# A conditioning product's last sum moved from the matrix engine to GpSimd, and its bias carried by another transposition

## The chip, the cores and the metric

The kernel runs on one core of a Trainium2 chip. The metric is the time of one execution on the device in microseconds (us); for a set of runs the median is given. Engines are named as the profile names them: PE (TensorE's matrix products), PEld (its weight loads, which overlap the products), DVE (VectorE), ACT (ScalarE), POOL (GpSimd), and SP (SyncE), which only issues transfers here. An entry such as SPq is the instruction queue of that engine. L482 is line 482 of the kernel.

## What is computed

One layer of a diffusion trunk with 1024 latent tokens, 256 context tokens and width 1024, all in float32. The part that matters here is the modulation: one vector of 6144 numbers, made from the conditioning vector `c`, that shifts, scales and gates the rest of the layer.

```python
mod = jax.nn.silu(c) @ ada_w[l] + ada_b[l]          # (1, 1024) @ (1024, 6144)
sh1, sc1, g1, sh2, sc2, g2 = jnp.split(mod, 6, axis=-1)
hx = modulate(rms_norm(x, norm1_g[l]), sh1, sc1)     # h * (1 + scale) + shift
out_x, _ = mixer_block(hx, lp, ctx_states, True)     # projection, conv group, RWKV group, projection
x = x + g1 * out_x
hx = modulate(rms_norm(x, norm2_g[l]), sh2, sc2)
x = x + g2 * conv_ffn(hx, lp, rows, GRID_W)
return rms_norm(x, final_g)
```

`sh1` and `sc1` are needed at once (and for the context tokens too). The other four, `g1, sh2, sc2, g2`, are needed later: `g1` at the output projection, `sh2` and `sc2` at the second normalization, `g2` at the very end.

## The kernel before, in words

The kernel works in stages: a start in which the inputs are normalized and `sh1, sc1` are made; the projections (`proj`, L354), in which each weight column block of 128 is multiplied in three passes of high and low halves; the decays and the inversion of small triangular matrices for the RWKV group (`decays`, `invert`); sixteen steps of the scan; the output projection; and the gated MLP (L1104, L1184).

Instructions are written in program order, and a planner in the framework lays them out at build time: it simulates the engines with its own costs and fixes the order in which each engine, and each engine's queue of transfers, will take its instructions. On the chip every engine keeps that order and waits at each instruction for what it needs. So an instruction that is planned too early holds up everything behind it on its engine, and a changed instruction can change the planned order elsewhere.

**The rest of the modulation** (`ada_rest`, L456 to L491) makes `g1, sh2, sc2, g2` in eight groups of 512 columns, numbered 4 to 11. It is a generator: the list `OR1` calls one group at a time between the column blocks of the first projections. For each group the 1024 rows of the weight come in as four transfers (`araw`, L466) of two row sets each. Row set k of the weight is multiplied by the k-th set of the conditioning vector and added to one of two accumulators of 128 x 512: accumulator 0 by DVE (L471, four additions; ACT makes the first product at L469), accumulator 1 by ACT and POOL (ACT scales, L473; POOL adds, L474, two additions). What is left is a sum over the 128 partitions, and over the two accumulators, which PE does with a vector of ones:

- in a **column group** (6 to 9: `sh2` and `sc2`) each 128 columns of each accumulator are loaded as weights and multiplied by the column of ones, and a third product adds the bias from a one-row tile `row`; the three accumulate in PSUM (L482, L483), and DVE copies the four columns out (L484). Every such float32 product shows as two records in the trace.
- in a **row group** (4, 5, 10, 11: `g1` and `g2`) the ones are the weights and the accumulators the moving data, 512 columns each (L487); DVE adds the bias row (L488), and the row goes to DRAM (L489).

The bias row is fetched by SP for all eight groups (L461) into `arow`, of which there are two.

**The small parameters** are fetched at the start by twelve transfers on POOL's queue (L278 to L290) into three blocks `pr` of 128 rows, which PE transposes (L292 to L294) and DVE copies into the tile `prm` (L295 to L299). Rows 78 to 93 of the first block are the bias of groups 0 to 3. `prm` is needed for the first modulation: L244, L255, then `gs1` (L316), then the modulated input (ACT L326), which the projections read.

`sp` (L104 to L106) splits a weight in two halves: ACT makes the high one, POOL the low one (`wlo`), which the projections use.

Of the kernel before, what the change touches and what calls it, by code (L numbers as in the profile page):

```python
# [8 lines left out]
F32 = mybir.dt.float32  # L9
F32R = mybir.dt.float32r  # L10
AF = mybir.ActivationFunctionType
ALU = mybir.AluOpType
# [25 lines left out]
PADC, PADM = 88, 80  # L38
# [49 lines left out]
def hybrid_kernel(  # L88
# [7 lines left out]
    V, A, G, PE, SY = nc.vector, nc.scalar, nc.gpsimd, nc.tensor, nc.sync  # L96

    PQ = G
# [9 lines left out]
    cp = ctx_.enter_context(tc.tile_pool(name="cp", bufs=1, side="left"))  # L108
# [18 lines left out]
    ident = cst[:, C_ID:C_ID + 128]  # L127


    prm = cp.tile([128, 292], F32, name="prm")  # L130
    P_N1, P_N2, P_KK, P_KA, P_RK, P_CW, P_FB, P_FW, P_LB, P_AB = 0, 8, 16, 20, 24, 28, 40, 62, 260, 276
    kac = cp.tile([128, 4], F32, name="kac")

    modc = cp.tile([128, 4, 8, 2], F32, name="modc")
# [2 lines left out]
    ccs = cp.tile([128, 8, 2], F32, name="ccs")  # L137
    eps6, epsg = 1e-6, 64e-5

    cp.tile([128, PADC], F32, name="padc")  # L140


    kd_ = dr.tile([4, 128, TT], F32, name="k_dram")
# [62 lines left out]
    with ExitStack() as s2:  # L206
# [15 lines left out]
        acc = [np_.tile([128, 512], F32, name=f"aacc{t}") for t in range(2)]  # L222
# [53 lines left out]
        pr = np_.tile([128, 3, 128], F32, name="pr")  # L276
        V.memset(pr, 0.0)
        PQ.dma_start(pr[0:8, 0, :], norm1_g[0].rearrange("(j p) -> j p", p=128))  # L278
        PQ.dma_start(pr[78:94, 0, :], ada_b[0, 0:2048].rearrange("(j p) -> j p", p=128))
        PQ.dma_start(pr[8:16, 0, :], norm2_g[0].rearrange("(j p) -> j p", p=128))  # L280
        PQ.dma_start(pr[16:20, 0, :], rw_k_k[0].rearrange("(j p) -> j p", p=128))
        PQ.dma_start(pr[20:24, 0, :], rw_k_a[0].rearrange("(j p) -> j p", p=128))
# [8 lines left out]
        pt = pp.tile([128, 512], F32, name="ptr", tag="pcol", bufs=1)  # L291
# [1 line left out]
        PE.transpose(pt[:, 128:256], pr[:, 1, :], ident)  # L293
        PE.transpose(pt[:, 256:384], pr[:, 2, :], ident)  # L294
        V.tensor_copy(prm[:, 0:62], pt[:, 0:62])  # L295
        V.tensor_copy(prm[:, P_AB:P_AB + 16], pt[:, 78:94])
        V.tensor_copy(prm[:, 62:161], pt[:, 128:227])
        V.tensor_copy(prm[:, 161:260], pt[:, 256:355])
        V.tensor_scalar(out=prm[:, P_LB:P_LB + 16], in0=pt[:, 62:78], scalar1=0.5, scalar2=None, op0=ALU.mult)  # L299
# [3 lines left out]
        for o in XO:  # L303
# [4 lines left out]
            else:  # L308
                ci = int(o)
                load_ada(ci, i_[ci])  # L310
                i_[ci] += 1
        while n_ < NT:
# [4 lines left out]
                               in1=prm[:, P_N1:P_N1 + 8].unsqueeze(2).to_broadcast([128, 8, 2]), op0=ALU.add, op1=ALU.mult)  # L317
        for g, (t0, n, w) in enumerate(segs3):
            for q in range(2):
                o = [seg_tile(g, q, i, F32R) for i in range(2)]  # L320
                hxt[g, q, 0], hxt[g, q, 1] = o
                for jj in range(4):
                    j = 4 * q + jj
# [43 lines left out]
    ad = sa.enter_context(tc.tile_pool(name="ad", bufs=1, side="right", reuse_waits="tile"))  # L367
# [88 lines left out]
    def ada_rest():  # L456
        kinds = {4: ("row", 0), 5: ("row", 0), 6: ("col", 2), 7: ("col", 2), 8: ("col", 3), 9: ("col", 3), 10: ("row", 1), 11: ("row", 1)}
        for ci in range(4, 12):
            src = ada_w[0, :, ci * 512:(ci + 1) * 512].rearrange("(p k) n -> p k n", k=8)
            row = ad.tile([1, 512], F32, name="arow", bufs=2)  # L460
            SY.dma_start(row, ada_b[0:1, ci * 512:(ci + 1) * 512])  # L461
            acc = [ad.tile([128, 512], F32, name=f"acc{e}", bufs=2) for e in range(2)]
            for k in range(8):
                if k % 2 == 0:
                    raw = ad.tile([128, 2, 512], F32, name="araw", bufs=AR)
                    SY.dma_start(raw, src[:, k:k + 2, :])  # L466
                e, z = AE[k], acc[AE[k]]
                if k == AE.index(e):
                    A.activation(z, raw[:, k % 2, :], AF.Identity, scale=ccs[:, k, 0:1])  # L469
                elif e == 0:  # L470
                    V.scalar_tensor_tensor(out=z, in0=raw[:, k % 2, :], scalar=ccs[:, k, 0:1], in1=z, op0=ALU.mult, op1=ALU.add)  # L471
                else:
                    A.activation(raw[:, k % 2, :], raw[:, k % 2, :], AF.Identity, scale=ccs[:, k, 0:1])  # L473
                    G.tensor_tensor(out=z, in0=z, in1=raw[:, k % 2, :], op=ALU.add)  # L474

            ps = pa_.tile([128, 512], F32, name="pada", tag="pa", bufs=2)
            one = cst[:, C_ONE:C_ONE + 1]
            half, (what, i) = ci % 2, kinds[ci]
            if what == "col":
                for b in range(4):  # L480
                    for e in range(2):
                        PE.matmul(ps[:, b:b + 1], acc[e][:, 128 * b:128 * b + 128], one, start=(e == 0), stop=False)  # L482
                    PE.matmul(ps[:, b:b + 1], row[:, 128 * b:128 * b + 128], one[0:1, :], start=False, stop=True)  # L483
                V.tensor_copy(modc[:, i, 4 * half:4 * half + 4, 0], ps[:, 0:4])  # L484
            else:
                for e in range(2):
                    PE.matmul(ps[0:1, :], one, acc[e], start=(e == 0), stop=(e == 1))  # L487
                V.tensor_tensor(out=row, in0=ps[0:1, :], in1=row, op=ALU.add)  # L488
                SY.dma_start(gd[i][:, 512 * half:512 * half + 512], row)  # L489
            yield  # L490
        V.scalar_tensor_tensor(out=gs2, in0=modc[:, 3, :, 0], scalar=1.0, in1=prm[:, P_N2:P_N2 + 8], op0=ALU.add, op1=ALU.mult)  # L491

    pa_ = Banks(pa=PA)
    ada_ = ada_rest()
    un = unit_k()
    for o in OR1.split():
# [558 lines left out]
    for r in range(16):  # L1055
# [3 lines left out]
        if r == RC:  # L1059
            fill(999)  # L1060
            sa.close()
            op = so.enter_context(tc.tile_pool(name="op", bufs=1, side="left", reuse_waits="tile"))
# [67 lines left out]
    for f in (1, 0, *range(2, NF)):  # L1130
# [12 lines left out]
        acc = up.tile([128, 16, 64], F32, name="acc", bufs=2)  # L1143
        for tap in range(9):
            a_, b_ = divmod(tap, 3)
# [9 lines left out]
        for hf, c0, n, t0 in PIECES:  # L1155
            V.tensor_tensor(out=act[:, t0:t0 + n], in0=pv[hf][:, c0:c0 + n],  # L1156
                            in1=acc.rearrange("p r c -> p (r c)")[:, t0:t0 + n], op=ALU.mult)
# [93 lines left out]
```

## Time and profile before

| | |
|---|---|
| median of 3 runs | 1708.09 us (1707.33 to 1716.09) |
| the profiled execution's own time | 1706.38 us |
| its span, first to last instruction | 1704.6 us |
| mean granted clock of TensorE | 0.94 of full |
| busiest engines over the span | PE 91%, DVE 67%, ACT 36%, POOL 33% |

The profile is of one execution of its own. Its time is 1.8 us more than the span, and the span is what the rows below divide. The busy shares are averages over stages with different limits, so the rows below are read by stage.

### The profile page before, as it was taken

What the parts mean: (1) busy time and instruction counts of PE and PEld (TensorE: products, weight loads), DVE (VectorE), ACT (ScalarE), POOL (GpSimd) and SP (SyncE); (2) the same over time, 40 slices, a digit from 0 to 9 for tenths busy, and PEclk for the clock granted to TensorE, in tenths of its full rate; (3) what the DMA queues carried; (4) which work ended last, traced back from release to release, by engine and by line L of the source; (5) the groups of instructions that cost most, each with busy time, mean ns of one, the idle gap of its engine ahead of it and who ended that gap; (6) DMA issues with size and microseconds to landing.
All of it is one profiled execution on the core that took longest, in us unless ns stands there. A gap on an engine that the chain in (4) does not pass through costs nothing.

```text
span 1704.6 us, 27504 instructions
## 1 busy us (share of the span) xinstructions
PE 1557.3 (91%) x10639; PEld 1258.8 (74%) x10639; DVE 1148.5 (67%) x1783; ACT 619.2 (36%) x1158; POOL 562.6 (33%) x489
## 2 busy tenths in 40 slices
PE   7699999989899866899778889999999999999997
PEld 2588768867777656787666668888888888788886
DVE  4954525798899987444677577777777777446645
ACT  2654315544445335444345331211111111324323
POOL 2343312332333303412444322222222222545643
PEclk9699799989799976999889999999999999999999
DMA  9385536557576487988652211111111111533521
GB/s 320 105 292 170 182 95 208 164 152 247 159 231 209 135 248 221 331 249 279 188 164 85 92 50 50 50 50 48 43 46 50 50 50 50 178 106 124 173 93 57
DMA packets 233147, 246.94 MB, mean 145 GB/s; under 512 B 18483, under 2 KB 171656, under 8 KB 233016
## 3 DMA queue, kind: packets, MB, share of 16 engines
q1 hardware_dynamic: 232632, 245.02, 46.1%
q8 instruction: 84, 1.38, 0.3%
q14 instruction: 47, 0.39, 0.1%
q0 software_dynamic: 384, 0.15, 0.0%
HBM read 178.79 MB, written 66.33 MB: 144 GB/s over the span
## 4 chain that ended last, share of the span: by engine, by line
PE 68%; DVE 17%; DMA 7%; ACT 3%; issue 3%; POOL 2%; SPq 1%; DVEq 0%; ACTq 0%; POOLq 0%
PE pf L1104 26%; PE pj L354 13%; PE pf L1184 12%; PE pco L906 2%; DVE ti L672 2%; DVE tmp L670 2%; PE po L906 2%; PE px L601 2%; DMA araw<-in_ada_w_dram 2%; DVE acc L1151 2%; PE ry L760 1%; PE pu L772 1%; PE ps L784 1%; DMA vu<-v_dram 1%; PE ry L752 1%
## 5 line engine op out<-in xcount | busy, mean ns | idle before, releaser
L1104 PE MATMUL pf<-h,fhi 128*128 128x512 f32 x1408 | 385.1, 390 | 6.7 <-DVE act L1156 4.1
L1104 PEld LDWEIGHTS pf<-h,fhi 128*128 128x128 f32 x1408 | 265.0, 188 | 63.1 <-DVE act L1156 4.5
L354 PE MATMUL pj<-hx,whi 128*128 128x512 f32 (+1 forms) x976 | 301.6, 388 | 0.9 <-DVE hx L328 0.9
L1151 DVE SCALAR_TENSOR_TENSOR acc<-gp,prm,acc 128x1024 f32<-128x1024 f32 x176 | 272.7, 1551 | 6.0
L106 POOL TENSOR_TENSOR flo<-fraw,fhi 128x1024 fp32r<-128x1024 f32 x50 | 124.2, 2485 | 306.0 <-ACT fhi L105 305.9
L1104 PE MATMUL pf<-h,flo 128*128 128x512 f32 x704 | 223.7, 390 | 0.0
L354 PEld LDWEIGHTS pj<-hx,whi 128*128 128x128 f32 x976 | 184.0, 196 | 37.2 <-issue 4.2
L354 PE MATMUL pj<-hx,wlo 128*128 128x512 f32 (+1 forms) x488 | 189.0, 388 | 0.0
L1184 PE MATMUL pf<-dhi,ahl 128*128 128x512 f32 x640 | 163.0, 389 | 0.2 <-DVE ahl L1176 0.2
L1176 DVE TENSOR_TENSOR ahl<-act,ahl 128x512 fp32r<-128x512 f32 x44 | 86.2, 1969 | 100.2 <-ACT ahl L1175 100.2
L1104 PEld LDWEIGHTS pf<-h,flo 128*128 128x128 f32 x704 | 132.5, 188 | 27.5 <-POOL flo L106 0.2
L105 ACT CAST fhi<-fraw 128x1024 fp32r<-128x1024 f32 x50 | 52.7, 1054 | 266.7 <-issue 158.6
L1184 PEld LDWEIGHTS pf<-dhi,ahl 128*128 128x128 f32 x640 | 120.0, 188 | 25.5 <-DVE ahl L1176 0.6
L106 POOL TENSOR_TENSOR dlo<-fraw,dhi 128x1024 fp32r<-128x1024 f32 x40 | 98.6, 2469 | 92.2 <-ACT dhi L105 88.2
L106 POOL TENSOR_TENSOR wlo<-wraw,whi 128x1024 fp32r<-128x1024 f32 x26 | 63.6, 2447 | 159.9 <-ACT whi L105 159.8
L354 PEld LDWEIGHTS pj<-hx,wlo 128*128 128x128 f32 x488 | 95.7, 196 | 17.2 <-issue 1.7
L1149 DVE TENSOR_SCALAR acc<-gp,prm 128x1024 f32<-128x1024 f32 x22 | 42.5, 1932 | 97.3 <-ACT gp L1141 97.3
L650 POOL TENSOR_TENSOR car<-car,pcs 128x512 f32<-128x512 f32 (+1 forms) x38 | 39.3, 1046 | 152.4 <-DMA car<-ar_dram 102.1
L1184 PE MATMUL pf<-dlo,ahl 128*128 128x512 f32 x320 | 89.1, 389 | 0.0
L601 PE MATMUL px<-arO,kbO 64*128 64x128 f32 (+1 forms) x640 | 63.9, 310 | 18.1 <-DVE xrO L605 12.7
L105 ACT CAST dhi<-fraw 128x1024 fp32r<-128x1024 f32 x40 | 41.9, 1050 | 105.0 <-PE pf L1184 87.4
L601 PEld LDWEIGHTS px<-arO,kbO 64*128 64x128 f32 x640 | 51.9, 207 | 34.6 <-issue 28.9
(292 smaller groups left out, 2651.2 us busy)
## 6 DMA issues: line engine op xcount, KB each, us to landing
araw<-in_ada_w_dram SPq DMA_DIRECT2D x48, 512.0 KB, 5.5
fraw<-in_ffn_w_up_dram SPq DMA_DIRECT2D x46, 512.0 KB, 3.8
fraw<-in_ffn_w_down_dram SPq DMA_DIRECT2D x44, 512.0 KB, 3.7
wraw<-in_w_in_dram SPq DMA_DIRECT2D x26, 512.0 KB, 4.5
lu<-lu_dram SPq DMA_DIRECT2D x20, 512.0 KB, 5.2
kb_dram<-kbT SPq DMA_DIRECT2D x40, 256.0 KB, 2.6
xa_dram<-xa SPq DMA_DIRECT2D x20, 512.0 KB, 5.6
cxa<-xa_dram SPq DMA_DIRECT2D x40, 256.0 KB, 3.8
```

Of the source, the lines that this page charges most:

```text
L105: A.copy(hi, src)
L106: G.tensor_tensor(out=lo, in0=src, in1=hi.bitcast(F32), op=ALU.subtract)
L354: PE.matmul(p[:, :n], w[:, k, :], hsl(i, k, t0, n), start=(k == 0 and first), stop=(k == 7 and last))
L601: PE.matmul(px[:, ch, i, 0:w], kbO[r, i, 2 * ch:2 * ch + 2, :].rearrange("p s n -> p (s n)"), rhs, start=True, stop=True)
L650: F3.tensor_tensor(out=self.ar, in0=self.ar, in1=self.pc.to_broadcast(list(self.ar.shape)), op=ALU.mult)
L670: V.tensor_tensor(out=tv, in0=ti[:, j + 1:32, j:j + 1].to_broadcast([128, m, j]), in1=ti[:, j:j + 1, 0:j].to_broadcast([128, m, j]), op=AL ...
L906: m = PE.matmul(po, hl[:, a_, k, :], w[k][b_][:, sl], start=(k == 0 and f), stop=(k == 3 and l))
L1104: PE.matmul(pts[hf], w[:, k, :], h2[hf][i_][:, k, :], start=(k == 0 and f), stop=(k == 7 and l))
L1149: V.tensor_scalar(out=acc, in0=src, scalar1=wcol, scalar2=prm[:, P_FB + f:P_FB + f + 1], op0=ALU.mult, op1=ALU.add)
L1151: V.scalar_tensor_tensor(out=acc, in0=src, scalar=wcol, in1=acc, op0=ALU.mult, op1=ALU.add)
L1176: V.tensor_tensor(out=hl[:, 1, :], in0=asl, in1=hl[:, 0, :].bitcast(F32), op=ALU.subtract)
L1184: PE.matmul(pd[i], hl[:, a_, 128 * q:128 * q + 128], w[w_][:, 512 * nh:512 * nh + 512], start=(f == 0 and s_), stop=(f == NF - 1 and l_))
```

## The change

POOL gets a third addition per group, which adds accumulator 1 to accumulator 0 when both are done. PE then sums one accumulator where it summed two. The column groups' bias, 2048 numbers, no longer comes as rows through SP and a third product: one more transfer on POOL's queue puts it in rows 94 to 109 of the first parameter block, it passes through the same transposition, the copy to `prm` is 32 columns wide where it was 16, and DVE adds it when it takes the four columns from PSUM. The row groups keep their bias row. `prm` grows by 16 columns and a padding tile shrinks by as many.

```diff
-    prm = cp.tile([128, 292], F32, name="prm")
+    prm = cp.tile([128, 308], F32, name="prm")
...
-    cp.tile([128, PADC], F32, name="padc")
+    cp.tile([128, PADC - 16], F32, name="padc")
...
         PQ.dma_start(pr[78:94, 0, :], ada_b[0, 0:2048].rearrange("(j p) -> j p", p=128))
+        PQ.dma_start(pr[94:110, 0, :], ada_b[0, 3072:5120].rearrange("(j p) -> j p", p=128))
...
-        V.tensor_copy(prm[:, P_AB:P_AB + 16], pt[:, 78:94])
+        V.tensor_copy(prm[:, P_AB:P_AB + 32], pt[:, 78:110])
...
         for ci in range(4, 12):
             src = ada_w[0, :, ci * 512:(ci + 1) * 512].rearrange("(p k) n -> p k n", k=8)
-            row = ad.tile([1, 512], F32, name="arow", bufs=2)
-            SY.dma_start(row, ada_b[0:1, ci * 512:(ci + 1) * 512])
+            half, (what, i) = ci % 2, kinds[ci]
+            if what == "row":
+                row = ad.tile([1, 512], F32, name="arow", bufs=2)
+                SY.dma_start(row, ada_b[0:1, ci * 512:(ci + 1) * 512])
...
+            G.tensor_tensor(out=acc[0], in0=acc[0], in1=acc[1], op=ALU.add)
...
             one = cst[:, C_ONE:C_ONE + 1]
-            half, (what, i) = ci % 2, kinds[ci]
             if what == "col":
                 for b in range(4):
-                    for e in range(2):
-                        PE.matmul(ps[:, b:b + 1], acc[e][:, 128 * b:128 * b + 128], one, start=(e == 0), stop=False)
-                    PE.matmul(ps[:, b:b + 1], row[:, 128 * b:128 * b + 128], one[0:1, :], start=False, stop=True)
-                V.tensor_copy(modc[:, i, 4 * half:4 * half + 4, 0], ps[:, 0:4])
+                    PE.matmul(ps[:, b:b + 1], acc[0][:, 128 * b:128 * b + 128], one, start=True, stop=True)
+                a_ = P_AB + 16 + 4 * (ci - 6)
+                V.tensor_tensor(out=modc[:, i, 4 * half:4 * half + 4, 0], in0=ps[:, 0:4], in1=prm[:, a_:a_ + 4], op=ALU.add)
             else:
-                for e in range(2):
-                    PE.matmul(ps[0:1, :], one, acc[e], start=(e == 0), stop=(e == 1))
+                PE.matmul(ps[0:1, :], one, acc[0], start=True, stop=True)
                 V.tensor_tensor(out=row, in0=ps[0:1, :], in1=row, op=ALU.add)
```

## Rows read from the trace of the kernel before

**Rows 1.** The page's engines: busy us, share of the span, instructions.

```profile
PE 1557.3 (91%) x10639; PEld 1258.8 (74%) x10639; DVE 1148.5 (67%) x1783; ACT 619.2 (36%) x1158; POOL 562.6 (33%) x489
```

**Rows 2.** Busy time by stretch (columns named in the first line).

```profile
core 0: us, PE busy (x) PEld busy (x) DVE busy (x) ACT busy (x) POOL busy (x), PEclk, DMA share, GB/s
0.00:76.00 76.00, 49.23 (x196) 27.12 (x197) 51.02 (x130) 32.32 (x61) 25.96 (x31) 0.82 0.73 232
...
76.00:250.00 174.00, 174.00 (x837) 135.14 (x836) 84.54 (x130) 69.41 (x118) 49.76 (x32) 0.93 0.55 176
...
250.00:314.00 64.00, 62.78 (x374) 51.12 (x373) 31.23 (x65) 31.36 (x61) 18.81 (x31) 1.00 0.68 208
314.00:600.00 286.00, 258.39 (x2188) 211.04 (x2188) 267.84 (x627) 135.38 (x256) 103.75 (x153) 0.92 0.60 184
```

**Rows 3.** Chain of waits, 76 to 314 us: shares of these 238 us by line.

```profile
by line: PE pj L354 73.4%; PE px L601 3.8%; PE pb L439 3.6%; PE pada L482 3.5%; PE pada L487 3.2%; PE psm L421 3.1%; PE pv L452 2.5%; PE pada L483 2.2%; PE pt L609 1.7%; PE plo L556 0.8%; PE plo L555 0.8%; PE prn L432 0.5%; PE pst L426 0.4%
```

**Rows 4.** Tile `pada`: instructions, duration in ns (min/median/max), starts, forms.

```profile
L482 PE MATMUL pada<-cst,acc x64: 164/250/352, 146.6 to 203.1; 128*128 128x1 f32 x64
...
L483 PE MATMUL pada<-cst,arow x32: 245/266/365, 147.0 to 203.6; 1*128 1x1 f32 x32
...
L487 PE MATMUL pada<-acc,cst x16: 590/592/954, 109.5 to 231.2; 128*1 128x512 f32 x16
...
L484 DVE COPY modc<-pada x4: 150/164/164, 149.9 to 204.2; 128x4 f32<-128x4 f32 x4
...
L244 DVE TENSOR_TENSOR modc<-pada,prm x1: 157/157/157, 40.0 to 40.0; 128x8 f32<-128x8 f32 x1
```

**Rows 5.** Timeline of PE: start us, us, what; in brackets the idle time before.

```profile
33.03 1.95 PE L243 MATMUL pada<-cst,aacc 128*128 128x1 f32 x16
34.84 0.31 PE L292 MATMUL ptr<-cst,pr 128*128 128x128 f32 x1
...
38.95 0.33 PE L294 MATMUL ptr<-cst,pr 128*128 128x128 f32 x1
...
44.79 3.68 PE L273 MATMUL ph<-cst,xt 128*128 128x128 f32 x16
...
109.49 1.88 PE L487 MATMUL pada<-acc,cst 128*1 128x512 f32 x4
...
229.42 1.02 PE L487 MATMUL pada<-acc,cst 128*1 128x512 f32 x2
```

**Rows 6.** Timeline of POOL.

```profile
7.77 0.57 POOL L290 DMA_DIRECT2D pr<-in_ffn_conv_w_dram  x1 [0.31 <-DMA pr<-in_rw_k_k_dram]
...
99.79 1.29 POOL L474 TENSOR_TENSOR acc<-acc,araw 128x512 f32<-128x512 f32 x1 [2.90 <-ACT araw L473]
...
118.10 2.41 POOL L106 TENSOR_TENSOR wlo<-wraw,whi 128x1024 fp32r<-128x1024 f32 x1 [3.24 <-ACT whi L105]
...
131.87 2.39 POOL L106 TENSOR_TENSOR wlo<-wraw,whi 128x1024 fp32r<-128x1024 f32 x1 [5.84 <-ACT whi L105]
```

**Rows 7.** Timeline of DVE and of ACT.

```profile
45.51 0.17 DVE L316 SCALAR_TENSOR_TENSOR gs<-modc,prm 128x16 f32<-128x16 f32 x1
...
118.68 2.38 DVE L471 SCALAR_TENSOR_TENSOR acc<-araw,ccs,acc 128x512 f32<-128x512 f32 x1 [4.97 <-ACT acc L469]
...
212.74 0.73 DVE L471 SCALAR_TENSOR_TENSOR acc<-araw,ccs,acc 128x512 f32<-128x512 f32 x1
...
46.28 2.07 ACT L326 ACTIVATE hx<-hx,modc,gs 128x256 fp32r<-128x256 f32 x4
```

**Rows 8.** SP's queue, 0 to 260 us: who waited for whom, us, times, longest.

```profile
SPq L461 <- PE pada L483: 6.1, 4, 2.5
```

**Rows 9.** Busy time by stretch, 160 to 220 us (columns as in group 2).

```profile
160.00:220.00 60.00, 60.00 (x271) 45.23 (x272) 28.72 (x52) 21.80 (x37) 16.88 (x11) 0.80 0.48 150
```

**Rows 10.** Transfers issued from 0 to 60 us: count, KB each, median us to landing.

```profile
pr<-in_ffn_conv_w_dram POOLq DMA_DIRECT2D x2, 49.5 KB, 5.4
```

## The prediction

> **What bounds the kernel now.** I read the page's busy shares first, then the busy time by stretch, then the chain of waits in the stretch where the changed lines run, and last the timelines around them. The shares alone [rows 1] say only that PE is the busiest engine and POOL is idle two thirds of the time. The stretches [rows 2] say more. From 76 to 250 us, where all eight groups of the rest of the modulation lie [rows 4], PE is busy 174.00 of 174.00 us; DVE works 84.54 of them and POOL 49.76. In the stretch after it, to 314, PE is busy 62.78 of 64. From 314 to 600 DVE takes over, 267.84 of 286.
>
> "Busy" is weak evidence for PE, because its records overlap. The chain of waits is stronger [rows 3]: over the 238 us from 76 to 314 every line with a share worth printing is a PE line. The three lines of the change take 3.5%, 2.2% and 3.2% of it. So PE's own queue sets the time here, and a product less on PE is time off the path. That makes this stretch unlike one where PE waits for data.
>
> **What comes off PE.** In us of the chain [rows 3]: L482 3.5% of 238 = 8.33; L483 2.2% = 5.24; L487 3.2% = 7.62; together 21.2.
>
> - The bias products (L483, 32 records) go entirely: 5.24.
> - Of the column groups' sums (L482, 64 records) half go: 4.16.
> - Of the row groups' sums (L487, 16 records) half go: 3.81.
>
> That is 13.2 us. A second way uses the only place where the trace already shows the new form, one float32 product of 128 x 128 with a single column, begun and ended by itself: L243, 16 records between 33.03 and the next product at 34.84 [rows 5], or 0.113 us a record, although each record is some 0.25 us long, as those of L482 are [rows 4]. The 32 column records that stay would take 3.62 us, so the column groups would drop from 13.57 to 3.62 and the sum would be 9.95 + 3.81 = 13.8. I take 13.2, which needs no other place's rate.
>
> **What is added.** POOL's eight additions are of the shape of L474, 1.29 us [rows 6]: 10.3 us on an engine that is idle 124 of the 174 us [rows 2]. They cost nothing if PE would come to the group's sum later than POOL is done. In group 4, the first, POOL's last addition ends at 99.79 + 1.29 = 101.08 and PE's sum starts at 109.49 [rows 5, 6]: 8.4 us of cover. In group 11, the last, DVE's last addition ends at 212.74 + 0.73 = 213.47 and PE's sum starts at 229.42 [rows 5, 7]: 16 us. Group 4 has the least cover of the eight. Were PE to come 12 us sooner at group 11 and DVE not, 4 us would be left, still more than 1.29. Without cover, one group would cost 1.29 us and eight 10.3. I take 0.
>
> Behind POOL's new addition on its queue stand the low halves of the weights (`wlo`, 2.41 us each [rows 6]), which the projections need. There are two buffers of each, so a half is made while PE still works through another block; two splits stand 13.8 us apart (118.10 and 131.87 [rows 6]), and a delay of 1.29 is hidden in that.
>
> DVE's last step of a column group becomes an addition of the same four columns with `prm`: 157 ns at L244 against 164 at L484 [rows 4]. Nothing. SP loses four small transfers and, with them, waits of its queue for PE to release `arow`, 6.1 us over four waits [rows 8], behind which weight and result transfers stood. SP is not on the chain here, so I count nothing for that either.
>
> **What is moved.** The start gets one transfer more on POOL's queue. The last of the twelve is issued at 7.77 and takes 5.4 to land [rows 6, 10], so all are there by about 13, or 14 with one more; PE transposes the blocks at 34.84 and 38.95 [rows 5]. On the data alone that is 21 us of cover. But PE's order is planned, and the three transpositions stand 4.11 / 2 = 2.05 us apart between other products, though their data had long landed: it looks as if the planner believes that these loads arrive one after another. One load more may push the three back by one such step. The path feels what exceeds the slack: `gs1` ends at 45.51 + 0.17 = 45.68 and ACT, busy until then, starts on it at 46.28 [rows 7], 0.6 us. So this costs 0 (no change of order) to 2.05 - 0.6 = 1.45. I take 1.4, because the even spacing speaks for the step. If they were pushed behind the whole group of 16 input transpositions that now starts at 44.79 and lasts 3.68 [rows 5], they would end about 9.5 us late, and 8.9 would reach the path.
>
> **The clock.** [...] No row shows that fewer one-column products would raise it, so I count 0, with -12 as an end; half as much again elsewhere, +6, is the other end.
>
> **Sum.** -13.2 + 1.4 = -11.8 us. Against the profiled execution's 1706.38 that is 1694.6; the median of the runs is 1.7 us above that execution, and the next median may fall on either side of this. I predict 1695.
>
> **Where the time goes afterwards.** The chain from 76 to 314 is one unbroken run of PE's queue, so what follows should start sooner by the whole amount. The next limit is DVE from 314: 267.84 of 286 us busy. Its work there begins with the decays, whose inputs PE makes, so it moves with PE.
>
> **Rivals.**
>
> *The gain is given back on the way.* Three rows allow it. (a) The late transpositions: 8.9 us instead of 1.4, total -4.3, 1702. (b) POOL's additions hold up DVE: at 118.68 an addition of DVE takes 2.38 us instead of 0.73, while POOL's split at 118.10 runs [rows 6, 7]. If all eight additions did this to DVE at a point where PE waits for it, 10.3 us would come back: total -1.5, 1705. Against it: DVE idles half of the stretch and is nowhere on the chain there. [...] (c) The 314 to 600 stage keeps its start, because transfers or another order hold it: part of the 13 is lost, 1700 to 1707. Together 0.26, nearly all of it within half a per cent of the time before.
>
> *Slower: PE waits for POOL.* The planner may place each group's product right where it believes POOL's addition ends; if on the chip that addition stands behind a split of 2.41 us in POOL's queue, PE stands for 2.41 + 1.29 = 3.7 us per group, 29.6 in all: 1694.6 + 29.6 = 1724. It decides from 11.8 / 8 = 1.5 us per group on (no gain), and from 2.5 on it is slower by half a per cent. Against it: the present 8 to 16 us of cover, and no wait of PE for accumulators in the trace. 0.10.
>
> *The clock comes back too.* -11.8 - 6 to -12: 1683 to 1689. 0.08.
>
> **How the numbers follow.** The forecast has 0.56, with its own range 1690 to 1699 (13.8 and no late step on one side, some of the 10.3 on the other). Half a per cent, 8.5 us, is about what a measurement of this kernel can tell from no change. Faster by more than that: the forecast and the clock, 0.64. Within it: 0.26. Slower: 0.10. A range that holds 8 in 10 takes in the middle of the clock's case and all but the top of the gain given back: 1686 to 1707.
>
> **What the changed profile would show.** Right: L482's and L487's successors with half the records and no record of a bias product; the products of the changed lines at 7 to 8 us of the chain where they had 21.2; PE still busy without a gap from some 76 us, and the last projections of the first set, now at 250, at about 238; the same distance shown at 314, 600 and the end. POOL's addition ending well before PE's product in all eight groups. Wrong: PE idle in front of the sums with POOL as releaser; the transpositions of the parameters after 41 us and the first modulated input after 47.7; DVE's start into the stage at 314 unmoved; or another granted clock than 0.80 in the middle of the projections.

## The result, and the profile after

The changed kernel took 1688.28 us, the median of 4 runs (1681.70 to 1689.85), against 1708.31 for the kernel before beside it: ratio 0.9875, 95% interval 0.9844 to 0.9906. Timed again it took 1685.10 (4 runs) against 1708.33: 0.9862, 0.9846 to 0.9878. So the change is worth some 20 to 23 us, clearly faster by the half per cent that this kernel's measurement can tell. The forecast was 1695 with 1690 to 1699 as its own range; the time came out where the third rival, the clock, had put it (1683 to 1689, with a chance of 0.08).

The profiled execution took 1681.70 us with a span of 1679.9. Busy time by stretch, in the columns of [rows 2]:

```profile
0.00:76.00 76.00, 49.54 (x196) 27.98 (x197) 51.30 (x130) 32.75 (x62) 27.32 (x32) 0.82 0.73 237
76.00:250.00 174.00, 171.61 (x864) 135.49 (x864) 88.38 (x137) 75.56 (x128) 64.53 (x44) 1.00 0.63 202
250.00:314.00 64.00, 64.00 (x402) 51.75 (x401) 42.30 (x84) 39.78 (x74) 23.01 (x38) 1.00 0.59 176
314.00:600.00 286.00, 253.51 (x2290) 205.07 (x2289) 267.28 (x620) 125.54 (x240) 91.23 (x144) 0.91 0.66 197
...
160.00:220.00 60.00, 58.17 (x310) 43.85 (x310) 32.33 (x59) 21.33 (x39) 22.02 (x15) 1.00 0.53 165
```

Two things are to be seen beside [rows 2, 9]. POOL works 14.8 us more from 76 to 250, its eight additions and two splits that have moved into the stretch, and PE still does not wait for it (its waits in the stretch end with DVE, 1.8 us, and ACT, 0.6). And the granted clock, 0.80 from 160 to 220 us before, is 1.00 throughout, though PE's busy time says nothing of the kind: 60.00 of 60 us before, 58.17 after.

The tile `pada`, as in [rows 4]; the bias products' line has no successor:

```profile
L484 PE MATMUL pada<-cst,acc x32: 164/250/271, 144.7 to 183.2; 128*128 128x1 f32 x32
...
L488 PE MATMUL pada<-acc,cst x8: 590/590/591, 109.3 to 206.1; 128*1 128x512 f32 x8
...
L486 DVE TENSOR_TENSOR modc<-pada,prm x4: 148/158/162, 145.7 to 187.6; 128x4 f32<-128x4 f32 x4
```

The timelines of PE, POOL and DVE, as in [rows 5 to 7]:

```profile
75.61 0.69 PE L355 MATMUL pj<-hx,whi 128*128 128x512 f32 x1
...
109.31 1.02 PE L488 MATMUL pada<-acc,cst 128*1 128x512 f32 x2
...
144.69 0.95 PE L484 MATMUL pada<-cst,acc 128*128 128x1 f32 x8
...
188.00 0.60 PE L433 MATMUL prn<-cst,rstd 128*8 128x128 f32 x4 [1.83 <-DVE rstd L175]
...
205.66 0.59 PE L488 MATMUL pada<-acc,cst 128*1 128x512 f32 x1
...
102.03 1.29 POOL L478 TENSOR_TENSOR acc<-acc,acc 128x512 f32<-128x512 f32 x1
...
192.76 1.29 POOL L478 TENSOR_TENSOR acc<-acc,acc 128x512 f32<-128x512 f32 x1
...
47.21 0.17 DVE L317 SCALAR_TENSOR_TENSOR gs<-modc,prm 128x16 f32<-128x16 f32 x1
```

In group 4 POOL's addition ends at 103.32 and PE's sum starts at 109.31, 6.0 us later; in group 11 it ends at 194.05 and PE starts at 205.66. The other six groups have more than 7 us. A column group's eight records now follow each other in 0.95 us where nothing stands between them (groups 6 and 7). The scale of the first modulation is 1.70 us later than before, 47.21 against 45.51 [rows 7].

Where the time was won shows best at the end of the first set of projections, when SP issues the last transfer of `v`. The row of the kernel before, and what PE began with at 75.8:

```profile
75.79 0.69 PE L354 MATMUL pj<-hx,whi 128*128 128x512 f32 x1
...
L454 SPq DMA_DIRECT2D v_dram<-stg x12: 359/368/379, 165.6 to 258.5; - x12
```

and of the kernel after, with the first instructions of the decays in both (before, after):

```profile
L455 SPq DMA_DIRECT2D v_dram<-stg x12: 359/366/425, 161.7 to 234.4; - x12
...
L555 PEld LDWEIGHTS plo<-dxl,lu x80: 186/190/338, 258.7 to 596.0; 128*128 128x128 f32 x80
...
L556 PEld LDWEIGHTS plo<-dxl,lu x80: 186/190/394, 245.8 to 580.1; 128*128 128x128 f32 x80
```

The start of the stretch is where it was (75.61 against 75.79), and the last transfer of `v` is 24.1 us sooner. PE has done nearly the same work by then: 645 records of projections stand between the start of the stretch and the last transposition for `v`, 647 before. The span of the profiled execution is 24.7 us shorter, so its gain stands at the end of this stretch. Behind that point the planned order is not the same: the decays follow 11.4 us after the transfer, where they followed 0.2 after it, because another column block of projections now comes first. Of these 24.1, PE's removed work is 13.2 by the prediction's own count; 60 x (1.00 - 0.80) = 12.0 is an estimate of the clock's part; and 2.4 us (174.00 - 171.61) go the other way, in waits of PE that did not exist before, the longest 1.83 us for DVE at 188.00. Together 22.8.

### The profile page after: what moved, and what is told of

Same layout as the page of the kernel before. It is cut to its first block, busy times and chain, and to the rows that moved or that the text cites. A ratio compares the mean times of both kernels' runs of the same rounds, so it can differ in the third digit from the quotient of the medians.

```text
span 1679.9 us, 27373 instructions
## 1 busy us (share of the span) xinstructions
PE 1534.4 (91%) x10567; PEld 1240.1 (74%) x10567; DVE 1154.1 (69%) x1783; ACT 619.9 (37%) x1158; POOL 567.3 (34%) x498
## 4 chain that ended last, share of the span: by engine, by line
PE 51%; DVE 13%; ACT 2%; DMA 2%; issue 2%; POOL 1%; SPq 0%; DVEq 0%; ACTq 0%; POOLq 0%
PE pf L1105 26%; PE pf L1185 13%; PE po L907 2%; PE pco L907 2%; DVE acc L1152 2%; PE pj L355 2%; DVE ti L673 2%; PE ry L761 2%; DVE tmp L671 1%; PE ps L785 1%; PE pu L773 1%; DMA car<-ar_dram 1%; PE ry L753 1%; DVE S L788 1%; PE ry L794 1%
## 5 line engine op out<-in xcount | busy, mean ns | idle before, releaser
L602 PE MATMUL px<-arO,kbO 64*128 64x128 f32 (+1 forms) x640 | 65.5, 308 | 13.2 <-DVE xrO L606 8.9
## 6 DMA issues: line engine op xcount, KB each, us to landing
kb_dram<-kbT SPq DMA_DIRECT2D x40, 256.0 KB, 4.3
cxa<-xa_dram SPq DMA_DIRECT2D x40, 256.0 KB, 4.2
```

The costliest lines, as they stand in the source:

```text
L602: PE.matmul(px[:, ch, i, 0:w], kbO[r, i, 2 * ch:2 * ch + 2, :].rearrange("p s n -> p (s n)"), rhs, start=True, stop=True)
```

## The experiments

Three theories were set against each other. Theory 1: PE's queue; the time follows the work taken off PE. Theory 2: the planner's changed order of the later stages makes the larger part of the gain. Theory 3: the clock; the one-column products held it down, and with two thirds of them gone (32 records where there were 96) 12 us come back on top. Theory 1 and 3 don't exclude each other.

**Only the bias part** (against the changed kernel: POOL's addition is left out).

```diff
-            G.tensor_tensor(out=acc[0], in0=acc[0], in1=acc[1], op=ALU.add)
...
-                    PE.matmul(ps[:, b:b + 1], acc[0][:, 128 * b:128 * b + 128], one, start=True, stop=True)
+                    for e in range(2):
+                        PE.matmul(ps[:, b:b + 1], acc[e][:, 128 * b:128 * b + 128], one, start=(e == 0), stop=(e == 1))
...
-                PE.matmul(ps[0:1, :], one, acc[0], start=True, stop=True)
+                for e in range(2):
+                    PE.matmul(ps[0:1, :], one, acc[e], start=(e == 0), stop=(e == 1))
```

> Only the bias part of the change: the bias comes through the parameters' transposition, POOL adds nothing, PE sums both accumulators as before. Theory 1, PE's queue: 32 of the 112 records are gone, 5.2 us by the chain of before, and whatever the clock gives back for them; 1696 to 1703 us. Theory 2, the changed order of the later stages gives the larger part of the gain and only needs some change of the program: anywhere between 1685 and 1708, not in proportion to PE's work. Theory 3, the one-column products hold the clock down and their number decides: the granted clock from 160 to 220 us is between 0.80 and 1.00.

1693.43 us (6 runs), 0.9908 (0.9892 to 0.9925): 15.5 us below the 1708.9 of before on that chip, three times the 5.2 of the products, and below the 1696 to 1703 that were expected from PE's queue. Its granted clock from 160 to 220 us is 0.97.

```profile
160.00:220.00 60.00, 60.00 (x318) 44.20 (x317) 31.03 (x59) 23.94 (x40) 20.30 (x12) 0.97 0.48 156
```

**Only POOL's addition** (against the kernel before).

```diff
+            G.tensor_tensor(out=acc[0], in0=acc[0], in1=acc[1], op=ALU.add)
...
-                    for e in range(2):
-                        PE.matmul(ps[:, b:b + 1], acc[e][:, 128 * b:128 * b + 128], one, start=(e == 0), stop=False)
+                    PE.matmul(ps[:, b:b + 1], acc[0][:, 128 * b:128 * b + 128], one, start=True, stop=False)
...
-                for e in range(2):
-                    PE.matmul(ps[0:1, :], one, acc[e], start=(e == 0), stop=(e == 1))
+                PE.matmul(ps[0:1, :], one, acc[0], start=True, stop=True)
```

> Only POOL's addition: PE sums one accumulator, and the column groups' bias is still fetched as a row and added by a third kind of product. Theory 1, PE's queue: 40 of the 112 records are gone (32 one-column, 8 wide ones), 8.0 us by the chain of before; 1692 to 1700 us. Together with the bias part alone the two gains make up that of the whole change, 20 us, within some 5 us. Theory 2, order: no such sum. Theory 3, clock: the granted clock from 160 to 220 us between 0.80 and 1.00.

1690.63 us (6 runs), 0.9888 (0.9868 to 0.9907), 18.3 us, again below what PE's queue alone was expected to give (1692 to 1700); the clock is 0.91.

```profile
160.00:220.00 60.00, 60.00 (x286) 44.54 (x285) 27.09 (x53) 19.88 (x34) 22.62 (x14) 0.91 0.46 146
```

The two halves make 33.7 us, the whole 20 to 23. Theory 1 alone had them add up to the whole within 5, and that fails. Theory 3 explains part of it: the clock's 12 us can be won once, and by the same estimate, 60 us x (clock less 0.80), the halves already win 10.2 and 6.6, together 4.8 too much. The rest of the surplus lies behind the first projections: at the last transfer of `v` the halves are 15.3 and 12.9 us ahead, together 28.2 against the whole's 24.1. Why POOL's half gains more behind that point is not shown.

**The products put back**, with everything else of the change left.

```diff
-                    PE.matmul(ps[:, b:b + 1], acc[0][:, 128 * b:128 * b + 128], one, start=True, stop=True)
+                    for _ in range(3):
+                        PE.matmul(ps[:, b:b + 1], acc[0][:, 128 * b:128 * b + 128], one, start=True, stop=True)
...
-                PE.matmul(ps[0:1, :], one, acc[0], start=True, stop=True)
+                for _ in range(2):
+                    PE.matmul(ps[0:1, :], one, acc[0], start=True, stop=True)
```

> The whole change, with PE's work put back: each column product is made three times and each row groups' product twice, on the same data, so that PE has about the number of records that it had before, while POOL's addition and the bias's new way stay. Theory 1, PE's queue: the gain is gone, 1703 to 1712 us. Theory 2, order: the gain stays, 1685 to 1692. Theory 3, clock: the granted clock from 160 to 220 us falls to about 0.80 again.

1704.12 us (12 runs, 1698.40 to 1712.13), 0.9979 (0.9962 to 0.9995). Most of the gain is gone with the work put back, and POOL's addition and the bias's way are still there. That speaks against theory 2, but does not close it, for the planner has made another order here too: the decays start 2.1 us after the last transfer of `v` (253.7 and 251.6). What speaks against it more is where the gain stands, ahead of the later stages. The clock is 0.89, lower than after, but not back at the 0.80 that theory 3 expected.

```profile
160.00:220.00 60.00, 60.00 (x298) 45.49 (x297) 27.41 (x52) 21.19 (x36) 20.55 (x14) 0.89 0.48 152
```

**Wide products in their place** (against the changed kernel), about as much time of PE in another form.

```diff
             if what == "col":
+                for _ in range(11):
+                    PE.matmul(ps, hsl(0, 0, 256, 128), hsl(0, 0, 256, 512), start=True, stop=True)
                 for b in range(4):
...
             else:
+                for _ in range(4):
+                    PE.matmul(ps, hsl(0, 0, 256, 128), hsl(0, 0, 256, 512), start=True, stop=True)
                 PE.matmul(ps[0:1, :], one, acc[0], start=True, stop=True)
```

> The whole change, with as much time of PE put back, but in wide products: eleven products of 128 x 512 in front of each column group's sum and four in front of each row group's, 60 in all of some 0.23 us, 13.8 us, which the sums then overwrite. Theory 1 without the clock: as the run with the products put back, 1703 to 1712 us. Theory 3, the one-column products hold the clock down: the clock stays at 1.00 from 160 to 250 us and only the 13.8 us come back, 1698 to 1704, some 6 to 12 us below the other. Theory 2, order: 1685 to 1692.

1696.92 us (6 runs, 1695.57 to 1702.04), 0.9930 (0.9910 to 0.9951), 7.2 us below the run before it, with an estimated 13 to 14 us of PE's time put back in each (13.2 by the prediction's count; 60 products of 0.23 us, as the 128 x 512 products of the projections follow each other, three in 0.68 us, 76.77 to 77.45 before). That is the difference that theory 3 expected (6 to 12), though the time itself is 1.1 us below its 1698 to 1704. The clock stays up:

```profile
160.00:220.00 60.00, 60.00 (x305) 45.46 (x304) 29.77 (x54) 21.42 (x37) 21.84 (x15) 1.00 0.49 153
```

**Are the clocks of single profiles worth anything?** Both kernels were profiled again, and later the two kernels with work put back.

> The kernel before, profiled a second time. If the low clock from 160 to 220 us belongs to the kernel, its granted clock there is 0.75 to 0.90 again and its span within 6 us of 1704.6. If it was an accident of one execution, the clock is 0.95 or more there, the span about 12 us shorter, and the theory that the one-column products hold the clock down loses its ground.

> The changed kernel, profiled a second time and timed in more rounds. The theory of the clock: 0.97 to 1.00 from 160 to 220 us again. The last projection of the first set, written 24.1 us sooner than before in the first profile, 20 to 25 sooner again; the time 1683 to 1691, and what the executions differ by lies behind 600 us.

> The change with the products put back, profiled again: granted clock from 160 to 220 us between 0.75 and 0.93, as in its first profile (0.89).

> The change with wide products in their place, profiled again: granted clock from 160 to 220 us of 0.97 or more, as in its first profile (1.00).

The kernel before, second profile: 1709.64 us, clock 0.77. Its span is 1707.9, 3.3 above the first.

```profile
160.00:220.00 60.00, 60.00 (x267) 45.81 (x265) 27.28 (x46) 21.31 (x35) 16.65 (x11) 0.77 0.44 140
```

The kernel after, second profile: 1685.65 us, clock 1.00, and the last transfer of `v` at 233.7, 24.8 us before that of the first profile of before.

```profile
160.00:220.00 60.00, 59.88 (x318) 45.32 (x317) 33.42 (x59) 21.84 (x39) 22.61 (x15) 1.00 0.53 165
```

The products put back took 1706.92 us in the second profile, with 0.83, the wide products 1692.72 with 1.00. So 0.77 to 0.80 before, 0.83 to 0.89 with the products back and 1.00 twice in each of the other two: in these four the low clock belongs to the kernel, not to the execution. The clocks of the two halves, and of the last experiment below, are from one profile each.

**Where the clock falls.** In slices of 2 us, the clock of the kernel before is, between 100 and 250 us, below 0.97 from 168 to 176, from 178 to 186 and from 202 to 214 us. Three of its column groups end around there; their last records, and the slices in which the clock falls:

```profile
168.19 0.41 PE L483 MATMUL pada<-cst,arow 1*128 1x1 f32 x2
...
179.69 0.58 PE L483 MATMUL pada<-cst,arow 1*128 1x1 f32 x2
...
203.36 0.58 PE L483 MATMUL pada<-cst,arow 1*128 1x1 f32 x2
...
166.00:168.00 2.00, 2.00 (x16) 1.94 (x16) 0.41 (x1) 0.52 (x2) 2.00 (x1) 1.00 0.23 66
168.00:170.00 2.00, 2.00 (x12) 1.97 (x12) 1.30 (x3) 1.80 (x3) 0.71 (x2) 0.60 0.00 1
...
178.00:180.00 2.00, 2.00 (x11) 1.73 (x10) 1.02 (x2) 0.63 (x1) 0.87 (x1) 0.66 0.13 49
...
202.00:204.00 2.00, 2.00 (x12) 1.94 (x10) 1.07 (x1) 1.85 (x4) 1.27 (x1) 0.64 0.59 176
```

The falls of the bias part alone (172 to 176), of POOL's addition alone (146 to 150, 166 to 172, 172 to 182) and of the products put back (170 to 174, 176 to 182, 196 to 204) begin in the last products of a column group or within 2 us behind them, too. Not every group is followed by one: the first group of the kernel before, 146.6 to 149.9, was not in the first profile, and was in the second (150 to 156; 0.83 from 150 to 160).

**POOL's addition twice.**

```diff
             G.tensor_tensor(out=acc[0], in0=acc[0], in1=acc[1], op=ALU.add)
+            G.tensor_tensor(out=acc[0], in0=acc[0], in1=acc[1], op=ALU.add)
```

> The changed kernel with POOL's addition made twice in each group, one after the other (so that its sums hold accumulator 1 twice): 1.29 us more in front of each of the eight sums and 10.3 us more of POOL. If PE's order leaves POOL the cover that the trace shows, the time is that of the changed kernel within 3 us. If PE waits for POOL, up to 10.3 us more, 1693 to 1699, with PE idle in front of the sums.

1685.09 us (4 runs) against 1685.10 of the changed kernel on the same chip. The second addition of group 4 ends at 104.90, PE's sum starts at 110.19:

```profile
101.84 1.29 POOL L478 TENSOR_TENSOR acc<-acc,acc 128x512 f32<-128x512 f32 x1
103.22 1.68 POOL L479 TENSOR_TENSOR acc<-acc,acc 128x512 f32<-128x512 f32 x1
...
110.19 1.02 PE L489 MATMUL pada<-acc,cst 128*1 128x512 f32 x2
```

Ten us more of POOL in the stretch cost nothing.

**One transfer for the bias.**

```diff
-        PQ.dma_start(pr[78:94, 0, :], ada_b[0, 0:2048].rearrange("(j p) -> j p", p=128))
-        PQ.dma_start(pr[94:110, 0, :], ada_b[0, 3072:5120].rearrange("(j p) -> j p", p=128))
+        PQ.dma_start(pr[78:118, 0, :], ada_b[0, 0:5120].rearrange("(j p) -> j p", p=128))
...
-        V.tensor_copy(prm[:, P_AB:P_AB + 32], pt[:, 78:110])
+        V.tensor_copy(prm[:, P_AB:P_AB + 32].rearrange("p (a b) -> p a b", b=16), pt[:, 78:126].rearrange("p (a b) -> p a b", b=24)[:, :, 0:16])
```

> The changed kernel with one transfer for the bias of all groups in place of two (40 rows, of which 8 are not used), so that POOL's queue has twelve transfers as before. If the transfer more is what the planner answers to, the three transpositions and the scale of the first modulation stand where they stood before, 45.5 us for the scale against 47.2. The theory that this step lies off the path: the time is that of the changed kernel within 3 us. If the late step cost 1.5 us, 1685 to 1688.

```profile
35.16 0.31 PE L292 MATMUL ptr<-cst,pr 128*128 128x128 f32 x1
...
37.21 0.33 PE L293 MATMUL ptr<-cst,pr 128*128 128x128 f32 x1
...
39.27 0.33 PE L294 MATMUL ptr<-cst,pr 128*128 128x128 f32 x1
...
45.44 0.17 DVE L316 SCALAR_TENSOR_TENSOR gs<-modc,prm 128x16 f32<-128x16 f32 x1
```

The transpositions stand between the other products again, in the order of before, and the scale is back at 45.44: it was the one transfer more that changed PE's order. The time is 1688.07 us (4 runs, 1685.99 to 1690.36) against 1685.10 of the changed kernel on the same chip, which had 1688.28 in its first timing; the last transfer of `v` is at 233.1, where the changed kernel has it at 234.4 and 233.7. The step cost nothing that shows, and taking it back gains nothing.

**Work added to the kernel before.** The sharpest test of theory 3: leave every one-column product of the kernel before and put wide products between them, three ahead of each 128 columns' share.

```diff
                 for b in range(4):
+                    for _ in range(3):
+                        PE.matmul(ps[:, 128:512], hsl(0, 0, 256, 128), hsl(0, 0, 256, 384), start=True, stop=True)
                     for e in range(2):
```

> The kernel before, with all its column products, and three wide products of 128 x 384 in front of each four output columns' share, so between the one-column products: 48 in all of some 0.18 us, 8.6 us of PE more, into columns that nothing reads. If the low clock comes from the stretches in which PE streams hardly any columns, the granted clock from 160 to 220 us rises to 0.95 or more, up to 12 us come back, and the kernel with more work is as fast as before or faster, 1702 to 1710 us. If the clock has another cause, it stays near 0.8 and the time is 1714 to 1720.

1710.67 us (12 runs, 1702.04 to 1720.49) against 1709.14 (17 runs): 1.0015, 0.9991 to 1.0038. The time is just outside the 1702 to 1710 of theory 3 and well short of the 1714 to 1720 of the other; the clock decides:

```profile
160.00:220.00 60.00, 60.00 (x329) 47.97 (x328) 29.80 (x54) 22.08 (x37) 17.06 (x12) 1.00 0.50 158
...
L482 PE MATMUL pada<-hx x48: 331/339/446, 147.0 to 206.3; 128*128 128x384 f32 x48
```

An estimated 8.6 us of PE's time (48 products at 0.18 us, between the 0.23 of 128 x 512 and the 0.12 of 128 x 256, three in 0.37 us, 146.32 to 146.69 after) were added to the engine that sets the pace, and no time that can be measured was lost (between 1.5 us less and 6.5 more). The profiled execution, 1702.45 us, is one of the two fastest of these twelve.

**The sum, run by run.** For each first profile: the work taken off PE by the prediction's count, the clock's part as 60 us x (its clock from 160 to 220 us less 0.80), and what the last transfer of `v` did against 258.5.

| kernel | work of PE | clock | sum | measured |
|---|---|---|---|---|
| whole change (2.4 us of new waits) | -13.2 | -12.0 | -22.8 | -24.1 |
| only the bias part | -5.2 | -10.2 | -15.4 | -15.3 |
| only POOL's addition | -8.0 | -6.6 | -14.6 | -12.9 |
| products put back | 0 | -5.4 | -5.4 | -6.9 |
| wide products in their place | +0.6 | -12.0 | -11.4 | -10.2 |
| before, with wide products between | +8.6 | -12.0 | -3.4 | -2.5 |

The measured column comes from each trace's row for that transfer. The changed kernel's stands above; the others, in the table's order:

```profile
L455 SPq DMA_DIRECT2D v_dram<-stg x12: 360/367/373, 165.0 to 243.2; - x12
...
L454 SPq DMA_DIRECT2D v_dram<-stg x12: 359/366/386, 164.0 to 245.6; - x12
...
L455 SPq DMA_DIRECT2D v_dram<-stg x12: 364/366/731, 166.1 to 251.6; - x12
...
L455 SPq DMA_DIRECT2D v_dram<-stg x12: 360/366/984, 166.3 to 248.3; - x12
...
L454 SPq DMA_DIRECT2D v_dram<-stg x12: 360/370/382, 168.3 to 256.0; - x12
```

No row is off by more than 1.7 us; in the one that is, POOL's addition alone, a fall of the clock from 146 to 150 us (0.98 from 76 to 160) lies outside the 60 us that the table counts. Among the second profiles the products put back are off by most, 2.2 us (254.5, clock 0.83). Two terms, both from rows, account for the end of the first projections in six kernels.

They do not account for all of the time behind it. The spans of the six profiles, against the 1704.6 of before, differ from the measured column by -7.7 (POOL's addition) to +4.5 us (wide products). Two profiles of one kernel, the wide products, differ in this by 6.9 us (+4.5 and -2.4), so an effect of a few us from the order of the later stages is neither seen nor ruled out.

## Why the prediction was right, and where it was not

*What bounds the kernel.* Right. PE's queue sets the time from 76 to 250 us; work put back on it in the same form came back in the time.

*What comes off PE.* The size, 13.2 us, fits within 2 us as one of the table's two terms. It can also be read at one clock, 1.00, between the changed kernel and the kernel before with wide products: their transfers stand 21.6 us apart (234.4 and 256.0), where 13.2 and 8.6, with 2.4 us of PE's waits in the one and 1.2 in the other, make 20.6. The second way of counting had 0.113 us a record, from the first start to the next product's; the same count gives eight records from 144.69 to 145.50, 0.101 each.

*What is added.* Right, and with room: POOL's additions are covered by 6 us or more in all eight groups, and twice as many cost nothing. The rival in which PE waits for POOL and the one in which POOL holds up DVE at a price find no support; the latter would have come out stronger with the doubled addition, and did not.

*What is moved.* One transfer more did change PE's order, as was feared, but not in the way that the sum describes, and its price was wrong. Two of the three transpositions moved by one step (36.67 and 38.73, where they stood at 34.84 and 36.88). The third, for which the copies of the parameters wait, did not: 38.90 against 38.95. What came later is the last of three sets of small products of the modulation (L254), because eight input transpositions (L273) were now put ahead of it. Before and after:

```profile
43.00 1.86 PE L254 MATMUL pcol<-cst,arows 2*128 2x2 f32 x8 [0.26 <-DVE modc L255]
...
38.90 0.27 PE L295 MATMUL ptr<-cst,pr 128*128 128x128 f32 x1
...
43.09 1.94 PE L273 MATMUL ph<-cst,xt 128*128 128x128 f32 x8 [0.35 <-DVE modc L255]
44.97 1.86 PE L254 MATMUL pcol<-cst,arows 2*128 2x2 f32 x8
```

So the scale came 1.70 us later and ACT's first modulated input 1.49 (47.77 against 46.28). That this is near the 1.45 foreseen is luck. Nor did it cost the 1.4 that the sum charged: PE comes to the next block of projections at 75.61, where it came at 75.79 before. Between 46 and 76 us PE waits for DVE's normalization of the other rows, and that did not move: PE's last such wait ends at 72.25 before and at 72.31 after. The slack had been taken at the first consumer, not at the point where the path picks the work up again.

*The clock.* This is the step that failed: "No row shows that fewer one-column products would raise it, so I count 0, with -12 as an end". It was a term of the sum set to zero that is worth as much as all the rest: 0.80 before, 1.00 after, an estimated 12 us. The measured time lies inside the stated range, 1686 to 1707, because the range held that end, and not because the likeliest case was right; the second timing, 1685.10, lies just outside. The prediction itself had named another granted clock than 0.80 as a sign of being wrong. No run shows the term by itself, with its ends of -12 and +6; what the runs showed in its place is the clock from 160 to 220 us, 0.80 [rows 9] and 1.00 after, from which the 12 is estimated (60 x 0.20). A row that bore on it had been read, [rows 9]: PE was busy 60.00 of 60 us at 0.80, so idle time in the records could not be the reason, and this stretch, where three of the four column groups lie (165.0 to 203.9), differed by them from its neighbours, which were at 1.00 with only the first (146.6 to 149.9):

```profile
76.00:160.00 84.00, 84.00 (x431) 68.80 (x431) 49.18 (x67) 44.32 (x76) 30.52 (x20) 1.00 0.70 231
...
220.00:250.00 30.00, 30.00 (x137) 21.11 (x136) 6.64 (x12) 3.28 (x6) 2.36 (x1) 1.00 0.24 75
```

The busy time of the records does not tell a clock of 0.80 from one of 1.00 here: 60.00 of 60 us is busy at 0.80 before and at 1.00 with wide products between.

*Where the time goes afterwards.* Right for the end, not for the way there. What was won by 250 us mostly reached the end: 24.1 us, and 24.7 of the span, in the first profile, 24.8 at the transfer against 20.7 of the span in the second (both against the first profile of before). But the distance is not the same all along, as the prediction had it: the decays start 12.9 us sooner, behind one more column block of projections, and the first weight load of the MLP comes 22.7 sooner (904.6 against 927.3). The last 4 us or so change from execution to execution behind 600 us, where the granted clock differs between executions of the same kernel (from 600 to 700 us 0.77 and 0.74 after, 0.64 and 0.71 with the wide products); what ties the one to the other was not tried.

## What to carry to other kernels

Where the profile shows PE busy without a gap at a low granted clock (here 60.00 of 60 us at 0.80), look at what its products are: a run of products with one moving column can cost more through the clock than through its own time, and taking out only part of it may give most of that back (here the bias products alone: 5.2 us of their own, and an estimated 10.2 by the clock, which rose from 0.80 to 0.97). Such a gain is won once, so the parts of a change can be worth more alone than together (here 33.7 us against 20 to 23). And a delay at the start is priced where the path next picks the work up, not at its first consumer (here 1.70 us at the scale, none at the projections, 75.61 against 75.79).

## What the runs showed of the hardware

- TensorE's granted clock fell to 0.77 and 0.80, as the mean of the 60 us from 160 to 220, in which PE's records leave no gap (60.00 of 60 us busy). In each of the kernels without the fall there were either fewer one-column products (32 records where there were 96) or wide products between them. What in these products does it, the single column, the float32 or their weight loads, no run separates.
- The falls begin around the end of a column group: in the 2 us from 168, from 178 and from 202, with groups that end at 168.6, 180.3 and 203.9. With eight records a group instead of 24 none was seen: the first profile after has 1.00 in every slice of 1 us from 100 to 250.
- Adding 48 products of 128 x 384 to that stretch, with all its one-column products left in, brought the clock to 1.00 from 160 to 220 us and cost no time that could be measured (1.0015, 0.9991 to 1.0038).
- A float32 product of 128 x 128 with one column shows as two records of about 0.25 us each, but eight such records pass in 0.95 us.
